# Regrouping a feed-forward layer that multiplies with seven products instead of eight

## The chip, the cores and the metric

The kernel runs on one core of one Trainium2 chip. The metric is device time in microseconds (us) of the whole program; the median of three runs before the change is 3438.2 us (3434.52 to 3442.72).

## The reference, cut to what matters

One layer of a hybrid decoder over 2048 prompt tokens and 64 sample tokens of width 1024, all in float32. The change touches the SwiGLU feed-forward that follows the output projection `h + mix @ w_out`:

```python
gu = rmsnorm(h, prm['norm2_g'][li]) @ prm['w_ffn_in'][li]
h = h + (jax.nn.silu(gu[..., :D_FF]) * gu[..., D_FF:]) @ prm['w_ffn_out'][li]
```

`D_FF` is 2816, that is 22 tiles of 128 features, each with a gate and an up part. After it come a gated per-layer input and a final norm.

## The kernel before

The prompt is worked on in four blocks of 512 tokens, counted from 0; block 3 also carries the 64 sample tokens. Everything is planned ahead: a scheduler simulates the program and fixes the order of instructions on each engine from priorities and data dependence, and tiles come from pools with a fixed number of buffers, whose reuse makes the next writer wait for the last reader. Token mixers (attention, recurrences) run beside the projections on the same engines, with lower priority. The sample tokens' mixers are placed beside block 2's last part.

Every matrix product is made of float32 operands split in a high part and a low rest (`split` L291 for activations, `unit` L268 and `parts` L688 for weights): ACT casts the high part, DVE or POOL subtracts it. Three matmuls (high-high, high-low, low-high) then replace one. High and low parts of weights live in two pools of seven buffers each, `whi` and `wlo` (L200, L201), raw weights in four buffers `wraw`. All weight loads are issued on SP's queue.

Blocks 0 and 1 use `rest` (L483), which the change leaves alone. Blocks 2 and 3 use `rest7` (L571): it splits the mixers' output (`mixed` L604), multiplies with `w_out` (`out_mm` L434, whose results are added to the residual rows h by DVE, L582), normalizes, runs the feed-forward `ffn7` (L622), and ends with a per-layer stage (L540).

`ffn7` splits the tokens in two halves (256 or 288 columns) and the 1024 rows of the contraction in two halves too, and computes gate and up of a feature tile together as a 2x2 block product. `seven` (L679) does that with seven block products instead of eight (twelve matmuls each, `prod` L712), from sums and differences of weights (four on DVE, L696) and of activations. The activations' sums are called t1 to t4, the plain blocks b11, b21, b12, b22. `Halves` (L103) makes them: PE transposes the scaled rows (L134), ACT multiplies by the gain into F (L139, L141), `split` makes the parts of the first token half; `second` (L153) makes those of the second half and t1 to t4 (subtractions on DVE, L164). Since t1 to t4 need both halves, the first feature tile is computed directly (`mm_half` L670, 96 matmuls): its first token half runs while the second is prepared. In one bank z, y or x a later product is added to an earlier one after DVE has read the earlier state:

```python
        prod(x, a11, ops["b11"], True)
        nc.scalar.copy(s, x)
        prod(z, s1, ops["t1"], True)
        tt(v, z, s, ALU.add)
        prod(y, s2, ops["t2"], True)
        tt(u, y, s, ALU.add)
        prod(x, a12, ops["b21"], False)
        prod(y, s3, ops["t3"], False)
```

After each feature tile ACT's tanh (L653) and two operations on DVE (L654, L655) give gate times up, and `split` (L296, L297) gives the tile `g`. Feature tiles are taken in groups: one tile first, then seven groups of three. After each group `out_mm` (matmuls on L364) multiplies the group's g with its rows of `w_ffn_out`, 512 output columns at a time, row tile by row tile, and DVE adds the result to h (L582). The last group's projection is interleaved with the norm of the per-layer stage.

Of the kernel before, what the change touches and what calls it, by code (L numbers as in the profile page):

```python
# [23 lines left out]
TB = 512  # L24
# [6 lines left out]
EPS = 1e-6  # L31
COL = {n: i * 256 for i, n in enumerate("aq af ai ag bq bk bv cq ck cv cz".split())}
# [4 lines left out]
class Norm:  # L37
# [33 lines left out]
    def steps(self):  # L71

        S, nc, acts, gain = self.S, self.S.nc, self.acts, self.gain
        for j, group in enumerate(self.groups):
# [6 lines left out]
            for k in range(KT):  # L81
                with S.at(0):
                    ps = S.bank()[:, :n]
                    for i, s in enumerate(xs):
                        nc.tensor.transpose(ps[:, i * rows:(i + 1) * rows], s[:, k * 128:(k + 1) * 128],  # L85
                                            S.ident[:rows, :rows])
                    S.split(acts[k][:, :, t0:t0 + n], ps, gain[:, k:k + 1])
                yield group[-1] if k == KT - 1 else None
# [14 lines left out]
class Halves(Norm):  # L103
# [4 lines left out]
    def __init__(self, S, h, gain, with_s, fp, sa):  # L108
# [3 lines left out]
        self.rows, self.ready, self.done = {}, {}, set()  # L112
        self.w = (TBS if with_s else TB) // 2
        self.f = [fp.tile([128, 2 * self.w], F32, name="F") for _ in range(KT)]
# [6 lines left out]
    def steps(self):  # L121
        S, nc, w = self.S, self.S.nc, self.w
        for j, group in enumerate(self.groups):
# [3 lines left out]
            for k in (0, 4, 1, 5, 2, 6, 3, 7):  # L127
                with S.at(0):
# [15 lines left out]
                yield  # L144

# [7 lines left out]
    def second(self, sb):  # L153
# [4 lines left out]
        nc = S.nc  # L158
        self.b22 = []

        self.b12 = [t[:, i] for t in (S.gp.tile([128, 2, 2, self.w], F32R, name="g", tag="g") for _ in range(2))
                    for i in range(2)]
        self.t = {n: [] for n in ("t1", "t2", "t3", "t4")}
        sub = lambda o, x, y: nc.vector.tensor_tensor(o, x, y, op=ALU.subtract)  # L164
        for k in range(4):
            b11, b12, b21, b22 = (self.part(a, j) for a, j in ((k, 0), (k, 1), (k + 4, 0), (k + 4, 1)))
            d = sb.tile([128, 2, self.w], F32R, name="Sb")
            self.b22.append(d)
            S.split(d, b22)
            tmp = S.xsp.tile([128, D], F32, name="xs")  # L170
            t1, t2, t3 = (tmp[:, i * self.w:(i + 1) * self.w] for i in range(3))
            sub(t1, b12, b11)
            sub(t3, b22, b12)
            sub(t2, b22, t1)
            S.split(self.b12[k], b12)
            sub(b21, b21, t2)
            for n, x in (("t1", t1), ("t2", t2), ("t3", t3), ("t4", b21)):
                d = sb.tile([128, 2, self.w], F32R, name="Sb")
                self.t[n].append(d)
                S.split(d, x)  # L180

    def half(self, j):
        if not j:
            return self.b11 + self.b21
        return self.b12 + self.b22

    def operands(self, sb):
        return {"b11": self.b11, "b21": self.b21, "b22": self.b22, **self.t}


class Step:
# [99 lines left out]
    def split(self, dst, src, scale=None):  # L291
# [3 lines left out]
        if scale is None:  # L295
            nc.scalar.copy(hi, src)  # L296
            nc.vector.tensor_tensor(lo, src, hi.bitcast(F32), op=ALU.subtract)  # L297
# [136 lines left out]
    def out_mm(self, acts, w, nk, n, with_s, use, norm=None, by_tile=False):  # L434
# [13 lines left out]
        for c, i, u in order:  # L448
            use(i, c, self.mm_a(acts, u, nk, i * 128, NS if i == 4 else 128, n))
# [121 lines left out]
    def rest7(self, b, mix, smix):  # L571
# [4 lines left out]
        w0 = (TBS if with_s else TB) // 2  # L576
# [7 lines left out]
        with pool("h7", 5 if with_s else 4) as self.hp, pool("g7", 3) as self.gp, ExitStack() as ops:  # L584
            ws, fp, sa = (ops.enter_context(pool(n, m)) for n, m in (("ws", 2), ("F", KT), ("Sa", KT)))
            with pool("pad", 1) as pad, pool("W", KT) as wp:
                if not with_s:
                    pad.tile([128, 1400], F32, name="pad")
# [4 lines left out]
                norm = Halves(self, h, self.gain["norm2_g"], with_s, fp, sa)  # L593
                self.out_mm(acts, I["w_out"][0], KT, 256, with_s, add, norm)
            last = self.ffn7(add, norm, ops.enter_context(pool("Sb", 20)), ws, with_s, w0)
            ops.close()
            with pool("L", KT) as lp:
# [3 lines left out]
                self.out_mm(*last, 512, with_s, add, norm, True)  # L601
# [20 lines left out]
    def ffn7(self, add, norm, sb, ws, with_s, w0):  # L622
# [3 lines left out]
        KC = 3  # L626
        f0 = 0
        while f0 < FT:
            n = KC if f0 else FT % KC
            gs = []  # L630
            for f in range(f0, f0 + n):
                wg, wu = (wi[:, c0:c0 + 128] for c0 in (f * 128, D_FF + f * 128))
                th = self.ev.tile([128, TBS], F32, name="ev")
                if f:
                    pairs = self.seven(wg, wu, ops, ws, w0)
                else:

                    us = [self.units([w], KT, 4) for w in (wg, wu)]
                    norm.first()
                    pairs = []  # L640
                    for j in range(2):
                        if j:
                            norm.second(sb)
                        if w0 == 256:
                            t = self.bank()
                            ps = [t[:, :w0], t[:, w0:]]
                        else:
                            ps = [self.bank()[:, :w0] for _ in us]
# [1468 lines left out]
```

## Time and profile before

| | |
|---|---|
| median of three runs | 3438.2 us |
| the profiled execution | 3437.55 us |
| its span, first to last instruction | 3435.7 us |
| mean granted TensorE clock | 0.978 |
| busy: PE / DVE / ACT / POOL | 3302.0 / 2254.7 / 1379.3 / 820.7 us |

PE is TensorE's matmuls, PEld its weight loads, DVE is VectorE, ACT is ScalarE, POOL is GpSimd, SP is SyncE, which issues the loads. L364 is line 364 of the kernel. An operation is written as output<-inputs, then its output and input shapes, then xN for a run of N. A figure in square brackets is idle time ahead of an instruction and what ended it. The granted clock is a share of 2.4 GHz. Times on PE are of pipelined matmuls, so starts tell more than durations.

### The profile page before, as it was taken

The numbers are of one execution on the slowest core, as the hardware profiler recorded it, in microseconds if no ns is written. First come the engines' busy times: TensorE is split into PE (matmuls) and PEld (weight loads), VectorE is DVE, ScalarE is ACT, GpSimd is POOL, SyncE is SP. The second block draws the span as 40 slices with busy tenths as digits, with TensorE's granted clock in tenths as the row PEclk, the third lists the DMA queues.
The fourth block names the chain that finished last, engine by engine and source line by source line (L and its number), as shares of the span: only waits on it lengthen the run. The fifth ranks groups of instructions, "written<-read, shape, count | busy, mean of one in ns | idle before, by whom it ended". The sixth has DMA issues, their size and how long they took to land.

```text
span 3435.7 us, 66579 instructions
## 1 busy us (share of the span) xinstructions
PE 3302.0 (96%) x24742; PEld 2815.2 (82%) x24742; DVE 2254.7 (66%) x6002; ACT 1379.3 (40%) x2931; POOL 820.7 (24%) x696
## 2 busy tenths in 40 slices
PE   7999999999999999998999999999999999899998
PEld 6788997888887778788878776787888889788988
DVE  4455566544577756688775455446799875877875
ACT  4433445324344224345333334535343453433443
POOL 2212122122112222212122212122334432233431
PEclk9999999999999999999999999999999999999999
DMA  6645445544433332534432443463533344122222
GB/s 207 181 121 149 127 123 155 148 125 145 129 109 118 101 96 87 132 91 146 113 103 81 124 114 110 143 215 113 162 102 88 91 129 134 60 81 90 83 89 79
DMA packets 621769, 411.92 MB, mean 120 GB/s; under 512 B 155357, under 2 KB 572877, under 8 KB 621445
## 3 DMA queue, kind: packets, MB, share of 16 engines
q1 hardware_dynamic: 618184, 405.12, 40.8%
q8 instruction: 195, 3.19, 0.4%
q10 hardware_dynamic: 3260, 2.55, 0.3%
q14 instruction: 130, 1.06, 0.1%
HBM read 348.77 MB, written 61.18 MB: 119 GB/s over the span
## 4 chain that ended last, share of the span: by engine, by line
PE 72%; DVE 13%; DMA 6%; SPq 4%; issue 3%; ACT 2%; POOL 1%; DVEq 0%; ACTq 0%; POOLq 0%
PE mmp L364 25%; PE mmp L344 22%; PE mmp L715 9%; SPq L1321 2%; PE acc L1852 1%; DVE c_X L1312 1%; DVE c_tmp L1310 1%; DMA wraw<-w_ffn_in 1%; DVE wlo L283 1%; PE mx L1135 1%; PE mx L1707 1%; PE mmp L85 1%; PE mx L1653 1%; PE mx L1764 1%; PE mx L1047 1%
## 5 line engine op out<-in xcount | busy, mean ns | idle before, releaser
L283 POOL TENSOR_TENSOR wlo<-wraw,whi 128x512 fp32r<-128x512 f32 (+1 forms) x356 | 497.5, 1399 | 1763.0 <-ACT whi L280 1112.8
L344 PE MATMUL mmp<-act,whi 128*128 128x512 f32 (+1 forms) x2944 | 892.7, 384 | 7.6 <-ACT ev L368 5.0
L280 ACT CAST whi<-wraw 128x512 fp32r<-128x512 f32 (+1 forms) x712 | 436.4, 619 | 667.4 <-PE mmp L344 240.6
L344 PEld LDWEIGHTS mmp<-act,whi 128*128 128x128 f32 x2944 | 532.9, 190 | 111.9 <-ACT ev L368 6.8
L364 PE MATMUL mmp<-whi,act 128*128 128x256 f32 (+3 forms) x2992 | 574.8, 290 | 11.8 <-DVE act L297 6.9
L344 PE MATMUL mmp<-act,wlo 128*128 128x512 f32 (+1 forms) x1472 | 554.0, 383 | 0.0
L364 PE MATMUL mmp<-whi,g 128*128 128x512 f32 (+1 forms) x1496 | 491.2, 406 | 15.4 <-DVE h L492 5.8
L364 PEld LDWEIGHTS mmp<-whi,act 128*128 128x128 f32 (+1 forms) x2992 | 470.8, 190 | 21.5 <-DVE act L297 7.8
L364 PE MATMUL mmp<-wlo,act 128*128 128x256 f32 (+2 forms) x1496 | 431.0, 289 | 0.2 <-DVE wlo L283 0.2
L283 DVE TENSOR_TENSOR wlo<-wraw,whi 128x512 fp32r<-128x512 f32 (+1 forms) x356 | 279.9, 787 | 219.0 <-ACT whi L280 198.3
L692 POOL TENSOR_TENSOR wlo<-wraw,whi 128x512 fp32r<-128x512 f32 x168 | 243.6, 1453 | 468.6 <-ACT whi L691 411.8
L364 PEld LDWEIGHTS mmp<-whi,g 128*128 128x128 f32 (+1 forms) x1496 | 273.3, 188 | 95.5 <-ACT g L296 8.5
L715 PE MATMUL mmp<-Sb,whi 128*128 128x256 f32 (+1 forms) x1680 | 328.0, 292 | 7.2 <-DVE xs L696 5.8
L344 PEld LDWEIGHTS mmp<-act,wlo 128*128 128x128 f32 x1472 | 276.4, 190 | 50.2 <-issue 2.0
L364 PE MATMUL mmp<-wlo,g 128*128 128x512 f32 x748 | 297.6, 400 | 0.0
L364 PEld LDWEIGHTS mmp<-wlo,act 128*128 128x128 f32 (+1 forms) x1496 | 283.5, 190 | 4.0 <-issue 2.0
L715 PEld LDWEIGHTS mmp<-Sb,whi 128*128 128x128 f32 x1680 | 267.0, 190 | 12.7 <-DVE xs L696 8.4
L715 PE MATMUL mmp<-Sb,wlo 128*128 128x256 f32 (+1 forms) x840 | 241.7, 291 | 1.8 <-POOL wlo L692 1.8
L691 ACT CAST whi<-wraw 128x512 fp32r<-128x512 f32 x210 | 128.8, 619 | 229.1 <-PE mmp L364 94.5
L364 PEld LDWEIGHTS mmp<-wlo,g 128*128 128x128 f32 x748 | 140.2, 187 | 33.7 <-issue 0.5
L715 PEld LDWEIGHTS mmp<-Sb,wlo 128*128 128x128 f32 x840 | 159.0, 190 | 3.4 <-POOL wlo L692 2.2
L582 DVE TENSOR_TENSOR h<-mmp,h 128x512 f32<-128x512 f32 (+3 forms) x180 | 107.6, 630 | 72.0 <-PE mmp L364 65.5
(472 smaller groups left out, 5250.1 us busy)
## 6 DMA issues: line engine op xcount, KB each, us to landing
wraw<-w_ffn_in SPq DMA_DIRECT2D x352, 256.0 KB
wraw<-w_in SPq DMA_DIRECT2D x208, 256.0 KB
wraw<-w_ffn_out SPq DMA_DIRECT2D x176, 256.0 KB
wraw<-w_out SPq DMA_DIRECT2D x64, 256.0 KB
wraw<-w_ple_gate SPq DMA_DIRECT2D x64, 256.0 KB
bs_K<-cache_b_k SPq DMA_DIRECT2D x48, 256.0 KB
xs<-x_prompt SPq DMA_DIRECT2D x16, 512.0 KB
h<-x_prompt SPq DMA_DIRECT2D x16, 512.0 KB
```

The lines of the kernel that those rows point to most:

```text
L85: nc.tensor.transpose(ps[:, i * rows:(i + 1) * rows], s[:, k * 128:(k + 1) * 128], S.ident[:rows, :rows])
L280: nc.scalar.copy(hi, raw)
L283: eng.tensor_tensor(lo, raw, hi.bitcast(F32), op=ALU.subtract)
L344: nc.tensor.matmul(ps, u[a], acts[k][:, b, t:t + w], start=i == 0, stop=i == n)
L364: nc.tensor.matmul(ps, acts[k][:, b, t0:t0 + rows], units[k][a], start=i == 0, stop=i == n)
L582: nc.vector.tensor_tensor(d, ps, d, op=ALU.add)
L691: nc.scalar.copy(hi, x)
L692: eng.tensor_tensor(lo, x, hi.bitcast(F32), op=ALU.subtract)
L715: nc.tensor.matmul(ps, w[a][:, k], op[k][:, b], start=first and k == 0 and j == 0, stop=k == 3 and j == 2, skip_group_check=True)
L1047: nc.tensor.matmul(ss[:, k:k + 2], x[:, c, t * m:(t + 1) * m], M.blk2, start=True, stop=True)
L1135: nc.tensor.matmul(ps[64 * hp:64 * hp + ms, ct, n], k[r, ct, 64 * n:64 * n + ms], part(q[r, ct, 64 * n:64 * n + 64], 1), start=True, stop= ...
L1321: nc.sync.dma_start(out=xt[r, ct, n], in_=xd[:, hp, ct, n, d].rearrange("k j i -> j k i"))
```

## The change

- The 22 feature tiles go in groups of 4, 5, 5, 5 and 3, and the first two (`LEAD`) are computed directly: first halves of both, then second halves of both.
- In `Halves`, the gain of rows 512 to 1023 is applied by DVE instead of ACT; the sample tokens stand in the middle of the columns, after row tile 1, so one operation scales a whole group of rows, and g is split by one pair of instructions. `out_mm` gets `mid`, which finds the row tiles there.
- `second` first splits b12 and b22 of all four k, then makes t1 to t4; the rest of t3 is subtracted by POOL; t4 takes t1's scratch.
- In `seven` the second product comes from t2 and the fourth from t1; the parts are made in another order, with s2 on DVE and a12 on POOL.
- The pool of F is shared with t1 to t4 of k = 2, 3; the pool `Sb` has 12 buffers instead of 20, the pool of g five instead of three; a padding tile is gone.

```diff
-    def __init__(self, S, h, gain, with_s, fp, sa):
+    ORDER = (0, 4, 1, 5, 2, 6, 3, 7)
+
+    def __init__(self, S, h, gain, with_s, sa, sf):
...
-        self.f = [fp.tile([128, 2 * self.w], F32, name="F") for _ in range(KT)]
+        self.f = {k: sf.tile([128, 2 * self.w], F32, name="F", tag="Sb") for k in self.ORDER}
...
-                    g, f = self.gain[:, k:k + 1], self.f[k]
-                    t0 = j * w
-                    m = w if n > 256 else 256
-                    nc.scalar.mul(f[:, t0:t0 + m], ps[:, :m], g)
-                    if n > m:
-                        nc.scalar.mul(f[:, 2 * w - n + m:], ps[:, m:], g)
+                    g, f = self.gain[:, k:k + 1], self.f[k][:, t0:t0 + n]
+                    if k < 4:
+                        nc.scalar.mul(f, ps, g)
+                    else:
+                        nc.vector.tensor_scalar_mul(f, ps, g)
...
+        new = lambda p: p.tile([128, 2, w], F32R, name="Sb", tag="Sb")
+        for k in range(4):
+            S.split(self.b12[k], self.part(k, 1))
+            self.b22.append(new(sb))
+            S.split(self.b22[k], self.part(k + 4, 1))
         for k in range(4):
             b11, b12, b21, b22 = (self.part(a, j) for a, j in ((k, 0), (k, 1), (k + 4, 0), (k + 4, 1)))
-            d = sb.tile([128, 2, self.w], F32R, name="Sb")
-            self.b22.append(d)
-            S.split(d, b22)
...
             sub(t1, b12, b11)
+            sub(t2, b22, t1)
             sub(t3, b22, b12)
-            sub(t2, b22, t1)
-            S.split(self.b12[k], b12)
-            sub(b21, b21, t2)
-            for n, x in (("t1", t1), ("t2", t2), ("t3", t3), ("t4", b21)):
-                d = sb.tile([128, 2, self.w], F32R, name="Sb")
-                self.t[n].append(d)
-                S.split(d, x)
+            for n, x in (("t1", t1), ("t2", t2), ("t3", t3), ("t4", t1)):
+                if n == "t4":
+                    sub(x, b21, t2)
+                self.t[n].append(new(sb if k < 2 else self.sf))
+                S.split(self.t[n][k], x, nc.gpsimd if n == "t3" else None)
...
-            use(i, c, self.mm_a(acts, u, nk, i * 128, NS if i == 4 else 128, n))
+            t0 = i * 128 if not mid or i < 2 else 256 if i == 4 else i * 128 + NS
+            use(i, c, self.mm_a(acts, u, nk, t0, NS if i == 4 else 128, n))
...
-        with pool("h7", 5 if with_s else 4) as self.hp, pool("g7", 3) as self.gp, ExitStack() as ops:
-            ws, fp, sa = (ops.enter_context(pool(n, m)) for n, m in (("ws", 2), ("F", KT), ("Sa", KT)))
-            with pool("pad", 1) as pad, pool("W", KT) as wp:
-                if not with_s:
-                    pad.tile([128, 1400], F32, name="pad")
+        with pool("h7", 5 if with_s else 4) as self.hp, pool("g7", 5) as self.gp, ExitStack() as ops:
+            ws, sa, sf = (ops.enter_context(pool(n, m)) for n, m in (("ws", 2), ("Sa", KT), ("Sf", KT)))
+            with pool("W", KT) as wp:
...
-            last = self.ffn7(add, norm, ops.enter_context(pool("Sb", 20)), ws, with_s, w0)
+            last = self.ffn7(add, norm, ops.enter_context(pool("Sb", 12)), ws, with_s)
...
+        for n in (4, 5, 5, 5, 3):
             gs = []
...
+            if not f0:
+
+                us = [[self.units([w], KT, 4) for w in cols(f)] for f in range(LEAD)]
+                norm.first()
+                pairs = [[] for _ in us]
+                for j in range(2):
+                    if j:
+                        norm.second(sb)
+                    for u, p in zip(us, pairs):
+                        p.append([self.mm_half(ps, w, norm.half(j)) for ps, w in zip(bank2(2), u)])
+                gs = [glu(p) for p in pairs]
+                ops = norm.operands()
+            gs += [glu(self.seven(*cols(f), ops, ws, w0)) for f in range(f0 + len(gs), f0 + n)]
             w = wo[f0 * 128:(f0 + n) * 128]
             f0 += n
             if f0 < FT:
-                self.out_mm(gs, w, n, 512, with_s, add)
+                self.out_mm(gs, w, n, 512, with_s, add, mid=with_s)
...
-        s1 = parts(s, V)
         tt(u1, g1, u1)
         tt(g1, s, g1)
-        s2 = parts(g1, G)
-        a12 = parts(g2, V)
+        s2 = parts(g1, V)
+        a12 = parts(g2, G)
+        s1 = parts(s, V)
...
-        x, z, y = (self.bank()[:, :w0] for _ in range(3))
+        x, y, z = (self.bank()[:, :w0] for _ in range(3))
...
-        prod(z, s1, ops["t1"], True)
-        tt(v, z, s, ALU.add)
         prod(y, s2, ops["t2"], True)
         tt(u, y, s, ALU.add)
         prod(x, a12, ops["b21"], False)
+        prod(z, s1, ops["t1"], True)
+        tt(v, z, s, ALU.add)
         prod(y, s3, ops["t3"], False)
```

## Rows read from the trace of the kernel before

**Rows 1.** The page, busy time, share of the span and instructions of each engine.
```profile
PE 3302.0 (96%) x24742; PEld 2815.2 (82%) x24742; DVE 2254.7 (66%) x6002; ACT 1379.3 (40%) x2931; POOL 820.7 (24%) x696
```
**Rows 2.** Busy time by stretches (us, PE, PEld, DVE, ACT, POOL, clock, DMA, GB/s).
```profile
2346.00:2396.00 50.00, 42.89 (x382) 34.10 (x383) 37.22 (x100) 33.93 (x79) 5.90 (x4) 0.93 0.35 102
2396.00:2787.00 391.00, 373.37 (x2800) 329.29 (x2798) 326.22 (x659) 162.16 (x324) 156.18 (x110) 0.99 0.41 116
2917.00:2960.00 43.00, 30.20 (x164) 25.56 (x164) 38.11 (x93) 25.13 (x69) 5.68 (x5) 0.80 0.13 37
2960.00:3345.00 385.00, 381.22 (x2388) 341.83 (x2388) 298.84 (x481) 154.46 (x310) 143.24 (x103) 1.00 0.29 87
```
**Rows 3.** PE's pace: stretches of 256 and 288 columns; timeline, 512 columns.
```profile
2880.00:2900.00 20.00, 20.00 (x172) 20.00 (x171) 5.83 (x12) 3.09 (x5) 2.92 (x2) 1.00 0.36 109
2960.00:2980.00 20.00, 20.00 (x152) 20.00 (x152) 14.47 (x24) 8.99 (x18) 9.30 (x7) 1.00 0.23 67
...
3171.03 0.39 PE L364 MATMUL mmp<-wlo,g 128*128 128x512 f32 x1
...
3179.36 0.62 PE L364 MATMUL mmp<-whi,g 128*128 128x512 f32 x2
```
**Rows 4.** Timeline of PE, two boundaries before a down projection in block 3.
```profile
3110.83 0.69 PE L364 MATMUL mmp<-whi,g 128*128 128x512 f32 x2 [0.17 <-ACT whi L691]
...
3166.45 0.70 PE L364 MATMUL mmp<-whi,g 128*128 128x512 f32 x2 [0.18 <-ACT whi L691]
...
3170.22 0.50 PE L364 MATMUL mmp<-whi,g 128*128 128x512 f32 x1 [0.38 <-DVE g L297]
```
**Rows 5.** Timeline of PE, block 3's opening: pauses, first seven-product tile.
```profile
2924.80 0.69 PE L134 MATMUL mmp<-ident,xs 128*128 128x128 f32 x2 [2.49 <-ACT F L141]
...
2928.32 1.97 PE L134 MATMUL mmp<-ident,xs 128*128 128x128 f32 x8 [2.83 <-DVE xs L68]
...
2946.10 0.40 PE L676 MATMUL mmp<-Sb,whi 128*128 128x288 f32 x1 [2.80 <-DVE Sb L297]
...
2949.74 3.35 PE L364 MATMUL mmp<-whi,g 128*128 128x512 f32 x7 [2.85 <-ACT g L296]
...
2959.16 0.43 PE L715 MATMUL mmp<-Sb,whi 128*128 128x288 f32 x2
```
**Rows 6.** Busy time by stretches within the two openings, columns as in rows 2.
```profile
2360.00:2370.00 10.00, 8.28 (x69) 6.48 (x70) 7.73 (x26) 6.12 (x16) 0.00 (x0) 0.66 0.31 90
...
2917.00:2930.00 13.00, 5.85 (x30) 4.13 (x29) 11.47 (x33) 10.02 (x31) 2.25 (x2) 0.65 0.21 61
...
2950.00:2955.00 5.00, 5.00 (x13) 3.77 (x13) 3.02 (x6) 0.00 (x0) 0.00 (x0) 0.51 0.27 77
```
**Rows 7.** Groups of instructions by shape, 2917 to 2946 (busy us, mean ns | idle).
```profile
L139 ACT ACTIVATE F<-mmp,gcol 128x288 f32<-128x288 f32 x8 | 3.7, 531 | 0.0
...
L141 ACT ACTIVATE F<-mmp,gcol 128x32 f32<-128x32 f32 x8 | 2.0, 339 | 0.0
...
L297 DVE TENSOR_TENSOR Sa<-F,Sa 128x288 fp32r<-128x288 f32 x8 | 3.4, 452 | 0.0
```
**Rows 8.** DVE's weight sums: one in the timeline, and their group (2960 to 3327).
```profile
3161.99 0.69 DVE L696 TENSOR_TENSOR ws<-wraw 128x512 f32<-128x512 f32 x1 [1.29 <-DMA wraw<-w_ffn_in]
...
L696 DVE TENSOR_TENSOR ws<-wraw 128x512 f32<-128x512 f32 x39 | 47.3, 1214 | 18.3 <-DMA wraw<-w_ffn_in 18.1
```
**Rows 9.** Block 2, 2396 to 2787: waits (total, times, longest); DVE's adds to h.
```profile
PE mmp L715 <- DVE xs L696: 5.5, 10, 1.7
...
PE mmp L364 <- ACT g L296: 1.1, 3, 0.5
...
L582 DVE TENSOR_TENSOR h<-mmp,h 128x512 f32<-128x512 f32 x54 | 35.1, 681 | 7.0 <-PE mmp L364 6.9
```
**Rows 10.** Groups of ACT and POOL, block 3's long stretch (2960 to 3327): weight parts.
```profile
L691 ACT CAST whi<-wraw 128x512 fp32r<-128x512 f32 x100 | 61.9, 620 | 126.1 <-PE mmp L364 57.9 <-issue 24.2 <-DVE wraw L696 19.7
...
L692 POOL TENSOR_TENSOR wlo<-wraw,whi 128x512 fp32r<-128x512 f32 x81 | 110.1, 1359 | 217.6 <-ACT whi L691 191.9 <-PE mmp L715 23.4 <-DVE wlo L692 1.9
```

More of the change, by code (lines that the diff above doesn't have):

```diff
@@ L86, in steps @@
                                             S.ident[:rows, :rows])
-                    S.split(acts[k][:, :, t0:t0 + n], ps, gain[:, k:k + 1])
+                    S.split(acts[k][:, :, t0:t0 + n], ps, scale=gain[:, k:k + 1])
                 yield group[-1] if k == KT - 1 else None
@@ L126, in steps @@
             n = sum(self.ready[i].shape[0] for i in group)
-            for k in (0, 4, 1, 5, 2, 6, 3, 7):
+            for k in self.ORDER:
                 with S.at(0):
@@ L157, in second @@
             pass
-        nc = S.nc
+        nc, w = S.nc, self.w
         self.b22 = []
-        self.b12 = [t[:, i] for t in (S.gp.tile([128, 2, 2, self.w], F32R, name="g", tag="g") for _ in range(2))
+        self.b12 = [t[:, i] for t in (S.gp.tile([128, 2, 2, w], F32R, name="g", tag="g") for _ in range(2))
                     for i in range(2)]
@@ L431, in in_proj, with out_mm @@
         return after
-    def out_mm(self, acts, w, nk, n, with_s, use, norm=None, by_tile=False):
+    def out_mm(self, acts, w, nk, n, with_s, use, norm=None, by_tile=False, mid=False):
         cols = [slice(c0, c0 + n) for c0 in range(0, D, n)]
@@ L600, in rest7 @@
                 norm = self.norm(lambda i: (h[i], False), self.gain["ple_norm_g"], with_s, scale=False, ahead=False)
-                self.out_mm(*last, 512, with_s, add, norm, True)
+                self.out_mm(*last, 512, with_s, add, norm, True, mid=with_s)
                 self.per_layer_out(b, h, norm, pa, pas)
@@ L620, in mixed, with ffn7, bank2, glu @@
         return acts
-    def ffn7(self, add, norm, sb, ws, with_s, w0):
+    def ffn7(self, add, norm, sb, ws, with_s):
         nc, I = self.nc, self.I
         wi, wo = I["w_ffn_in"][0], I["w_ffn_out"][0]
-        KC = 3
+        w0 = norm.w
+        def bank2(n):
+            if 2 * w0 > TB:
+                return [self.bank()[:, :w0] for _ in range(n)]
+            t = [self.bank() for _ in range((n + 1) // 2)]
+            return [t[i // 2][:, i % 2 * w0:(i % 2 + 1) * w0] for i in range(n)]
+        def glu(pairs):
+            th = self.ev.tile([128, TBS], F32, name="ev")
+            for j, (gate, up) in enumerate(pairs):
+                e = th[:, j * w0:(j + 1) * w0]
+                nc.scalar.activation(e, gate, AF.Tanh, scale=0.5)
+                nc.vector.scalar_tensor_tensor(e, e, 1.0, gate, op0=ALU.add, op1=ALU.mult)
+                nc.vector.scalar_tensor_tensor(e, e, 0.5, up, op0=ALU.mult, op1=ALU.mult)
+            g = self.gp.tile([128, 2, 2 * w0], F32R, name="g", tag="g")
+            self.split(g, th[:, :2 * w0])
+            return g
+        cols = lambda f: [wi[:, c0:c0 + 128] for c0 in (f * 128, D_FF + f * 128)]
@@ L627, in ffn7 @@
         f0 = 0
-        while f0 < FT:
-            n = KC if f0 else FT % KC
+        for n in (4, 5, 5, 5, 3):
             gs = []
[L631 to L648, printed above, removed]
-                        pairs.append([self.mm_half(p, u, norm.half(j)) for p, u in zip(ps, us)])
-                    ops = norm.operands(sb)
-                for j, (gate, up) in enumerate(pairs):
-                    e = th[:, j * w0:(j + 1) * w0]
-                    nc.scalar.activation(e, gate, AF.Tanh, scale=0.5)
-                    nc.vector.scalar_tensor_tensor(e, e, 1.0, gate, op0=ALU.add, op1=ALU.mult)
-                    nc.vector.scalar_tensor_tensor(e, e, 0.5, up, op0=ALU.mult, op1=ALU.mult)
-                g = self.gp.tile([128, 2, 2 * w0], F32R, name="g", tag="g")
-                gs.append(g)
-                halves = th[:, :2 * w0].rearrange("p (j n) -> p j n", j=2)
-                for c, m in ((0, 256), (256, w0 - 256)):
-                    if m:
-                        self.split(g[:, :, 2 * c:2 * (c + m)].rearrange("p a (j n) -> p a j n", j=2),
-                                   halves[:, :, c:c + m])
```

22 lines of the change are left out of this document (11 added, 11 removed).

## The prediction

> **What bounds the kernel now.** I read the page's busy times first, then busy time by stretches of the part that the change touches, then the timeline at PE's pauses, then waits and instruction groups. The page says that PE is busy for 96% of the span and no other engine for over 66% [rows 1]. The change touches only the two blocks that use seven products. Blocks are counted from 0: block 2 runs its feed-forward from 2346 to 2787 us, block 3 (with the sample tokens) from 2917 to 3345. So only what PE loses in these 870 us can come back. In four stretches [rows 2] the reader is to see that losses sit in the two openings (7.1 us idle of 50 in block 2, 12.8 of 43 in block 3) and in block 2's long stretch (17.6 of 391), while block 3's long stretch is nearly full (3.8 of 385).
>
> Busy time hides a second loss: a matmul counts as busy while it is slow. So I take PE's undisturbed pace [rows 3]: 172 matmuls of 256 columns in 20 us (0.1163 us each), 152 of 288 columns in 20 us (0.1316), and 36 starts of 512 columns from 3171.03 to 3179.36 (0.2314). With these, one period of three tiles in block 3 should take 252 x 0.1316 + 90 x 0.2314 = 54.0 us; the timeline shows 55.6 from one boundary to the next (3110.83 to 3166.45) [rows 4]. The missing 1.6 us lie where PE turns from a seven-product tile to the down projection and waits for the last tile's g. There are six such boundaries per block, and a seventh before the last projection.
>
> In block 3's opening [rows 5] PE waits 2.49 us for ACT's F, 2.83 for the scaled rows xs, 2.80 for an operand part Sb and 2.85 for the first g. Right after these pauses the granted clock is 0.65 and 0.51 of 2.4 GHz, that is near the 1.2 GHz level, and in block 2's opening 0.66 [rows 6]: ten microseconds at 2360 hold 69 matmuls.
>
> **The change, part by part.** The sum is made against the profiled execution, 3437.55 us (span 3435.7), which is 0.65 below the median of the runs.
>
> *Second direct tile.* A direct tile has 96 matmuls, a seven-product tile 84. Twelve more cost 12 x 0.1163 = 1.4 us in block 2 and 1.6 in block 3. What it buys is cover: first halves of two tiles instead of one (96 matmuls, 12.6 us in block 3) run while second-half operands are made.
>
> *Opening of block 3.* Before, the norm part takes 13 us (2917 to 2930) with ACT busy 10.0 and DVE 11.5 [rows 6]. ACT loses its eight 32-column scalings (0.34 each) and four of the wide ones (0.53) [rows 7], 4.8 us; DVE gains four scalings. Those aren't shown on DVE; the nearest rows are its other 288-column operations at 0.45 [rows 7], so 2 us, against which weight sums at 0.69 [rows 8] move behind the direct tiles. ACT alone would give 4 us, DVE alone might cost 1; I take 1 us gained, since DVE has the fewer free slices. Then 192 direct matmuls, 25.3 us. DVE was busy 38.1 of the 43 us [rows 2] and still has nearly all of it to do, so I leave 3 us of waiting before the first seven-product tile (0 to 6). It would start at 2917 + 12 + 25.3 + 3 = 2957.3. Before, it starts at 2959.16 [rows 5] with one direct tile and its 30 down matmuls done; put on equal work that is 2959.16 + 84 x 0.1316 - 30 x 0.2314 = 2963.3. Gain 6 us, the extra matmuls within it. With ACT's 4 us and no waiting it would start at 2951.3, with DVE's 1 us of loss and 6 of waiting at 2962.3: bounds 12 and 1.
>
> *Opening of block 2.* It loses 7.1 us idle [rows 2] and some 3 to the low clock [rows 6], partly from the sample mixers, which stay. I take 4 of these back, bounds 0 and 8, minus the 1.4 us of matmuls.
>
> *Groups of 4, 5, 5, 5, 3.* Two boundaries fewer per block. Block 3: 2 x 1.6 = 3.2 us, bounds 0 and 9 (a longer group has more k steps to do before the last g is needed, so the others may shrink too). In block 2 waits on g are 1.1 us in three [rows 9]: I take 1 us, bounds 0 and 2. Evacuations fall by 24 per block in block 2 and 30 in block 3, 0.68 us of DVE each [rows 9]. In block 3 that hides under PE. In block 2 DVE is busy 326 of 391 us [rows 2] and PE's longest list of waits there is for DVE's sums xs (5.5 us in 10) [rows 9]. 16 us of adds and some 6 of weight work go; I take 4 us back, bounds 0 and 8. The first projection's two loads of 256 KB move on SP's queue behind those of three more tiles, where they are needed later too; POOL's queue is passed by nothing.
>
> *Order of products, engines of the parts.* Nothing. The bank y has one product more of cover before its third product, z three fewer before its last; each order has two one-product covers. DVE and POOL make as many parts as before. If DVE's queue is late, z is what waits next, at the 0.5 us a wait of [rows 9]. *Sample tokens in the middle*: one split per g instead of two, 22 short pairs less on ACT and DVE, hidden beside PE except at the boundaries already counted. *Pools*: operands of k = 2, 3 take over the buffers of F, whose last readers stand ahead of them on DVE; no wait, and if one came it would hold only DVE's split for 0.45 us.
>
> *Third operands' parts go from DVE to POOL.* A DVE subtraction of weights takes 0.69 us alone, but 1.21 on average beside POOL's parts (1.36 each) [rows 8, 10]. I count neither gain nor loss (bounds 2 us either way, inside the opening's). The Trainium skill ("SBUF — State Buffer", Who interferes with whom) says that a VectorE instruction with two SBUF inputs blocks fully against a GpSimd one that reads SBUF; the trace's stretched mean agrees, and by that rule the move would relieve DVE of nothing.
>
> Sum: -6 - (4 - 1.4) - 3.2 - 1 - 4 = -16.8; 3437.55 - 16.8 = **3420.8 us**.
>
> **Rivals.**
> *DVE is the bound of the openings.* For: 38.1 of 43 us busy, and the subtractions held by POOL. Against: PE's pauses name ACT and PE's own queue order too. The openings would give 1 us in block 3 and nothing in block 2, DVE no relief: 3437.55 - 1 - 3.2 - 1 + 1.4 = 3433.8. The Trainium skill's rule on the shared port (above) would lead here.
> *All waits of these kinds go.* The upper ends, shaved by a quarter since they don't add up fully: 12 + 8 + 9 + 2 + 8 - 1.4 = 37.6, so 28 us, 3409. For: block 2's DVE load falls by 7%. Against: sample mixers' waits stay.
> *Seven weight buffers are too few* (the slow side). Two direct tiles need eight pairs of whi and wlo where there are seven, a projection of five tiles ten, one of four eight; before, six. For the second column half, the third part can only be made once the last row tile of the first half lets go of its first. PE then has 18 matmuls of cover, 4.2 us; ACT's cast plus POOL's subtraction take 0.62 + 1.36 [rows 10], so it decides where a cast starts over 2 us late. ACT's casts already wait for PE [rows 10]. Price: 2 us at each of two turns in eight groups, 32 us, giving 3437.55 - 16.8 + 32 = 3453; slower from 12 of the 16 turns on. Against: the output projection before (256-column stretch of [rows 3]) also refills its buffers in flight, and runs without a pause.
> *It doesn't do what it says*: PE's order is fixed ahead of the run, and if it puts the second halves where they were, all stays at about 3437.
>
> **How the numbers follow.** My forecast has 0.55, DVE's bound 0.18, all waits 0.12, the buffers 0.10, no effect 0.05. A measurement of this kernel can tell 0.2% (6.9 us) from no change, so faster means below 3431.3. The forecast's own range, with two of its larger terms at their ends, is 3411 to 3430. Faster: 0.55 + 0.12 + a third of DVE's case (it lies 2.5 us above the line) = 0.73. Same: the other two thirds and no effect, 0.17. Slower: the buffers, 0.10. The range reaches from 3406 (all waits) to 3434 (DVE's case); the buffers, no effect and a tail of the lower case are left out.
>
> **What would show it.** Right: no pause over 1 us before the first seven-product tile of block 3, which starts some 41 us after its last output projection; two direct tiles ahead of it; a granted clock of 1.00 there; four boundaries of some 1.6 us; fewer waits for xs in block 2. Wrong: waits of PE on whi or wlo in the middle of a down projection (buffers), DVE without idle time in the opening and PE waiting for Sb ahead of the seven products (DVE's bound), or a start of block 3 that is no earlier than before.

## The result, and the profile after

The changed kernel takes 3471.0 us (median of four runs, 3462.7 to 3476.7). The kernel before took 3438.2 beside it. The ratio is 1.0093 [1.0067, 1.0119], so the change costs 0.9% where a gain of 0.5% was forecast. The profiled execution took 3476.67 us. The page of the changed kernel, span and busy times:

```profile
span 3474.9 us, 66460 instructions
...
PE 3321.5 (96%) x24766; PEld 2827.4 (81%) x24766; DVE 2205.7 (63%) x5914; ACT 1362.8 (39%) x2877; POOL 819.6 (24%) x700
```

Against [rows 1] DVE has 49 us less to do and PE 24 matmuls more, as foreseen, and still the span is 39 us longer. (9.6 of it lie ahead of block 2's norm, where no instruction changed; see the last section.) The stretches that answer to [rows 2], same columns: opening and seven products of block 2, then of block 3.

```profile
2356.00:2408.00 52.00, 47.28 (x442) 40.38 (x443) 37.35 (x98) 32.27 (x72) 13.39 (x9) 0.93 0.35 101
2408.00:2799.00 391.00, 365.67 (x2699) 318.88 (x2698) 300.70 (x614) 152.73 (x309) 146.01 (x106) 0.97 0.38 109
2934.00:2981.50 47.50, 39.26 (x281) 37.63 (x280) 42.56 (x113) 26.16 (x62) 13.63 (x9) 0.89 0.11 32
2981.50:3367.00 385.50, 365.22 (x2265) 326.29 (x2264) 257.77 (x396) 138.19 (x261) 138.31 (x99) 1.00 0.28 85
```

The openings improved: PE is idle 4.7 and 8.2 us where it was 7.1 and 12.8, although they now hold two direct tiles. The long stretches are where the time went: in block 3 PE now idles 20.3 of 385.5 us, before 3.8 of 385, while DVE's busy share there falls from 78% to 67%. PE's waits between the first and the last seven-product matmul of block 3 (total, times, longest), after the change:

```profile
PE mmp L715 <- DVE xs L696: 18.8, 17, 2.6
PE mmp L715 <- POOL wlo L692: 1.1, 3, 0.6
PE mmp L367 <- DVE ev L640: 0.3, 1, 0.3
```

and the same view of the kernel before:

```profile
PE mmp L364 <- DVE g L297: 1.9, 5, 0.4
PE mmp L364 <- ACT whi L691: 0.9, 5, 0.2
PE mmp L715 <- DVE xs L696: 0.3, 1, 0.3
```

20.2 us against 3.1. From its first seven-product matmul to the end block 3 takes 3474.9 - 2981.5 = 493.4 us; before it took 3435.7 - 2959.2 = 476.5, on equal work (one tile of 11.05 us less, 30 down matmuls of 0.2314 more) 472.4. So 17.1 of the 21.0 us lost are these waits. PE waits for DVE's adds of a product out of a bank (xs), although DVE is less loaded.

For the lines that follow: a tile's four raw weight buffers hold two gate blocks g1, g2 and two up blocks u1, u2. DVE makes s = u1 + u2, then u1 = g1 - u1 and g1 = s - g1 in place, and later s = g2 - g1 in the same buffer s (pool `ws`). The parts (ACT's high cast, and the low rest on DVE or POOL) of the first s are s1, of the new g1 s2, of the new u1 s3, of the second s s4; a12 and a22 are those of g2 and u2. DVE's timeline over one tile of block 3 shows what stands ahead of the adds:

```profile
3162.08 0.69 DVE L696 TENSOR_TENSOR ws<-wraw 128x512 f32<-128x512 f32 x1 [1.35 <-DMA wraw<-w_ffn_in]
3162.69 0.45 DVE L696 TENSOR_TENSOR xs<-mmp,xs 128x288 f32<-128x288 f32 x1
...
3163.42 0.68 DVE L696 TENSOR_TENSOR wraw<-wraw 128x512 f32<-128x512 f32 x1
3164.21 0.69 DVE L696 TENSOR_TENSOR wraw<-ws,wraw 128x512 f32<-128x512 f32 x1
...
3166.22 1.77 DVE L692 TENSOR_TENSOR wlo<-wraw,whi 128x512 fp32r<-128x512 f32 x1
3167.91 1.77 DVE L692 TENSOR_TENSOR wlo<-ws,whi 128x512 fp32r<-128x512 f32 x1
3169.61 0.45 DVE L696 TENSOR_TENSOR xs<-mmp,xs 128x288 f32<-128x288 f32 x1
3169.97 0.68 DVE L696 TENSOR_TENSOR ws<-wraw 128x512 f32<-128x512 f32 x1
3171.39 0.69 DVE L692 TENSOR_TENSOR wlo<-ws,whi 128x512 fp32r<-128x512 f32 x1 [0.74 <-ACT whi L691]
...
3176.26 0.83 DVE L696 TENSOR_TENSOR ws<-wraw 128x512 f32<-128x512 f32 x1 [1.83 <-DMA wraw<-w_ffn_in]
...
3177.38 0.44 DVE L696 TENSOR_TENSOR xs<-mmp,xs 128x288 f32<-128x288 f32 x1
```

PE's pauses in the same microseconds, and POOL's rests beside the two long ones of DVE:

```profile
3163.19 0.53 PE L715 MATMUL mmp<-Sb,whi 128*128 128x288 f32 x2 [1.69 <-DVE xs L696]
...
3170.11 0.53 PE L715 MATMUL mmp<-Sb,whi 128*128 128x288 f32 x2 [1.27 <-DVE xs L696]
...
3177.88 0.40 PE L715 MATMUL mmp<-Sb,whi 128*128 128x288 f32 x1 [1.64 <-DVE xs L696]
...
3166.15 2.98 POOL L692 TENSOR_TENSOR wlo<-wraw,whi 128x512 fp32r<-128x512 f32 x2 [4.09 <-ACT whi L691]
```

Read it as a round. 3162.08 is the first sum, u1+u2, which waited for its load. The two other sums follow, then the rests of s2 and s1, 1.77 us each, and only then, at 3169.97, the difference g2-g1 (also `ws<-wraw`): it is written into s, which s1's parts still read. The difference gives the raw buffers of g1 and g2 back; the loads of the next tile follow, and its first sum starts at 3176.26. That is 7.89 us from sum to difference, 6.29 from difference to sum, a round of 14.2 us; the two rounds before it in this group take 12.4 and 13.4. PE needs 84 x 0.1316 = 11.05 us for a tile [rows 3]. Each time DVE stands at the sum for a load, or in the two long rests, an add queued behind it comes late and PE pauses: of the 17 waits, 11 (13.1 us) end with an add that stands behind a sum that waited for its load, and six (5.7 us) with one right behind the two rests. That the loads wait for the difference shows on SP's queue, over the same stretch of block 3, after and then before the change:

```profile
SPq L685 <- DVE ws L696: 173.8, 14, 18.0
```

```profile
SPq L685 <- DVE ws L696: 91.4, 13, 9.0
```

The same three instructions in the kernel before:

```profile
3128.05 0.69 DVE L696 TENSOR_TENSOR ws<-wraw 128x512 f32<-128x512 f32 x1 [1.00 <-DMA wraw<-w_ffn_in]
...
3132.31 1.74 DVE L696 TENSOR_TENSOR ws<-wraw 128x512 f32<-128x512 f32 x1
...
3140.10 1.11 DVE L696 TENSOR_TENSOR ws<-wraw 128x512 f32<-128x512 f32 x1 [0.22 <-DMA wraw<-w_ffn_in]
```

There the difference comes 4.26 us after the sum, since s1's parts are made second, and the round is 12.05 us.

### The profile page after: what moved, and what is told of

Read it like the earlier page. It is cut to its first block, busy times and chain, and to the rows that moved or that the text cites. A ratio compares the mean times of both kernels' runs of the same rounds, so it can differ in the third digit from the quotient of the medians.

```text
span 3474.9 us, 66460 instructions
## 1 busy us (share of the span) xinstructions
PE 3321.5 (96%) x24766; PEld 2827.4 (81%) x24766; DVE 2205.7 (63%) x5914; ACT 1362.8 (39%) x2877; POOL 819.6 (24%) x700
## 5 line engine op out<-in xcount | busy, mean ns | idle before, releaser
L367 PE MATMUL mmp<-whi,g 128*128 128x512 f32 (+1 forms) x1496 | 484.0, 403 | 8.7 <-DVE h L496 5.3
L715 PE MATMUL mmp<-Sb,whi 128*128 128x256 f32 (+1 forms) x1600 | 319.4, 296 | 30.5 <-DVE xs L696 28.2
L692 POOL TENSOR_TENSOR wlo<-wraw,whi 128x512 fp32r<-128x512 f32 x160 | 228.2, 1433 | 391.3 <-ACT whi L691 318.9
L367 PE MATMUL mmp<-wlo,g 128*128 128x512 f32 (+1 forms) x748 | 296.5, 399 | 0.0
L715 PEld LDWEIGHTS mmp<-Sb,whi 128*128 128x128 f32 x1600 | 255.2, 192 | 42.9 <-DVE xs L696 37.8
L715 PE MATMUL mmp<-Sb,wlo 128*128 128x256 f32 (+1 forms) x800 | 229.8, 292 | 0.0
L691 ACT CAST whi<-wraw 128x512 fp32r<-128x512 f32 x200 | 120.8, 618 | 194.9 <-DVE wraw L696 92.8
L367 PEld LDWEIGHTS mmp<-wlo,g 128*128 128x128 f32 (+1 forms) x748 | 139.4, 186 | 34.5 <-POOL wlo L286 0.4
L585 DVE TENSOR_TENSOR h<-mmp,h 128x512 f32<-128x512 f32 (+3 forms) x126 | 74.2, 608 | 90.5 <-PE mmp L367 81.8
## 6 DMA issues: line engine op xcount, KB each, us to landing
xs<-x_prompt SPq DMA_DIRECT2D x16, 512.0 KB
h<-x_prompt SPq DMA_DIRECT2D x16, 512.0 KB
```

The source lines that it names most:

```text
L367: nc.tensor.matmul(ps, acts[k][:, b, t0:t0 + rows], units[k][a], start=i == 0, stop=i == n)
L585: nc.vector.tensor_tensor(d, ps, d, op=ALU.add)
L691: nc.scalar.copy(hi, x)
L692: eng.tensor_tensor(lo, x, hi.bitcast(F32), op=ALU.subtract)
L715: nc.tensor.matmul(ps, w[a][:, k], op[k][:, b], start=first and k == 0 and j == 0, stop=k == 3 and j == 2, skip_group_check=True)
```

## The experiments

Single profiles are compared by stages, because spans shift (last section): the time from the first norm transposes of block 2 to those of block 3, and from there to the end. `xs` is PE's wait for DVE's adds in block 3's seven products (us). Each ratio is to runs of the kernel before on the same chip at the same time, whose medians lay between 3438.2 and 3441.9 us.

| kernel | median us | ratio to before | block 2 | block 3 to end | xs |
|---|---|---|---|---|---|
| before | 3438.2 | 1 | 563.0 | 525.8 | 0.3 |
| after | 3471.0 | 1.0093 [1.0067, 1.0119] | 577.3 | 541.1 | 18.8 |
| e1_groups3 | 3457.7 | 1.0045 [1.0029, 1.0062] | 573.6 | 530.3 | 8.6 |
| e2_oldorder | 3447.9 | 1.0021 [1.0007, 1.0034] | 574.0 | 518.8 | 2.3 |
| e3_groups3_oldorder | 3435.8 | 0.9971 [0.9957, 0.9985] | 561.3 | 518.4 | 0 |
| e4_before_neworder | 3462.6 | 1.0055 [1.0033, 1.0076] | 570.6 | 531.2 | 5.6 |
| e5_before_newparts | 3445.8 | 1.0019 [1.0007, 1.0030] | 571.0 | 522.6 | 0.3 |
| e6_before_newproducts | 3431.1 | 0.9970 [0.9956, 0.9984] | 559.2 | 518.8 | 0.5 |
| e8_after_sum_on_pool | 3477.2 | 1.0109 [1.0091, 1.0127] | 582.9 | 544.7 | 24.8 |
| e9_own_diff | 3437.1 | 0.9983 [0.9966, 1.0] | 560.0 | 523.2 | 5.6 |
| e10_own_raw | 3458.6 | 1.0045 [1.0027, 1.0062] | 570.0 | 535.9 | 13.0 |
| e12_oldparts | 3440.1 | 1.0001 [0.9988, 1.0014] | 569.5 | 522.9 | 4.9 |
| e11_groups3_oldparts | 3431.2 | 0.9976 [0.9964, 0.9988] | 569.1 | 512.0 | 0 |
| e14_old_engines | 3468.2 | 1.0081 [1.0063, 1.0099] | 579.7 | 539.2 | 19.4 |
| e17_new_engines | 3437.7 | 0.9994 [0.9980, 1.0007] | 567.7 | 519.4 | 0.5 |
| e15_own_diff_groups3 | 3423.6 | 0.9948 [0.9930, 0.9965] | 559.0 | 513.0 | 0 |
| e16_groups3_oldparts_own | 3433.6 | 0.9976 [0.9964, 0.9987] | 570.5 | 512.6 | 0 |

**Which part of the change.** Four kernels take the groups and the two orders in `seven` (parts and products together) back, one by one and both, and put the new orders alone into the kernel before. The edits:

```diff
# e1 and e3: groups
-        for n in (4, 5, 5, 5, 3):
+        for n in (4, 3, 3, 3, 3, 3, 3):
# e2 and e3: parts and products as before (e4: the reverse, in the kernel before)
         tt(s, u1, u2, ALU.add)
+        s1 = parts(s, V)
...
-        s2 = parts(g1, V)
-        a12 = parts(g2, G)
-        s1 = parts(s, V)
+        s2 = parts(g1, G)
+        a12 = parts(g2, V)
...
-        x, y, z = (self.bank()[:, :w0] for _ in range(3))
+        x, z, y = (self.bank()[:, :w0] for _ in range(3))
...
+        prod(z, s1, ops["t1"], True)
+        tt(v, z, s, ALU.add)
         prod(y, s2, ops["t2"], True)
...
-        prod(z, s1, ops["t1"], True)
-        tt(v, z, s, ALU.add)
```

> The changed kernel with its feature tiles in groups of 4 and then six times 3; all else as changed. Theory 1 (a run of five seven-product tiles outruns the preparation of its weights, which a down projection every three tiles lets catch up): the 33 us lost in the seven-product stretches go, some 5 us come back for two more boundaries per block, so about 3443 us, and PE's waits for xs in block 3 fall from 18.8 us to under 5. Theory 2 (the new order of the parts makes the preparation of one tile longer, whatever the grouping): it stays above 3460.

> The changed kernel with parts and products of a seven-product tile in the order of before; groups of 4, 5, 5, 5, 3 kept. Theory 1 (length of the runs): hardly faster than the changed kernel, 3462 to 3471 us, waits for xs in block 3 above 12 us. Theory 2 (order of the parts): back to about 3438 us, and the last group, which has three tiles and lost some 5 us, runs as before.

> Both undone: groups of 4 and six times 3, old order of parts and products; the two direct tiles, the openings, the sample tokens in the middle and the pools stay as changed. If run length and order together are the whole loss, what is left is the openings' gain (5.7 us in block 3 and 1.4 in block 2, by the traces) and one boundary fewer per block: about 3428 to 3432 us. If something else of the change costs time (pools, the upstream part), it stays above 3438.

> The kernel before with only the new order of parts and products. Theory 1: within 4 us of before, 3434 to 3442. Theory 2: slower by 10 us or more, with waits for xs inside the groups of three.

The orders cost most: undone they give 0.7% in groups of five (e2), and alone they make the kernel before 0.55% slower (e4). The groups cost too, with either order. What is left without both (e3: openings, second direct tile, sample tokens in the middle, pools) is 0.3% faster than before. The undone groups (e1) gave less than the first of the two expectations and more than the second; e2 came back most of the way.

**Parts or products.** e5 and e6 split e4.

```diff
# e5: parts only, in the kernel before
-        s1 = parts(s, V)
...
-        s2 = parts(g1, G)
-        a12 = parts(g2, V)
+        s2 = parts(g1, V)
+        a12 = parts(g2, G)
+        s1 = parts(s, V)
# e6: products only, in the kernel before
-        x, z, y = (self.bank()[:, :w0] for _ in range(3))
+        x, y, z = (self.bank()[:, :w0] for _ in range(3))
...
-        prod(z, s1, ops["t1"], True)
-        tt(v, z, s, ALU.add)
         prod(y, s2, ops["t2"], True)
...
         prod(x, a12, ops["b21"], False)
+        prod(z, s1, ops["t1"], True)
+        tt(v, z, s, ALU.add)
```

> The kernel before with only the new order and engines of a tile's weight parts (s1 fourth, s2 on DVE, a12 on POOL); products in the old order. Theory A (the parts: the sum for s2 and the longer hold of raw buffers put DVE's weight sums ahead of their loads, and PE's xs sums wait behind them): most of the 20 us of the whole order, 3450 us or more on a chip where before is 3440, and DVE's waits for w_ffn_in in block 3 at 30 us or more (18 before). Theory B (the products: less cover for a bank's second use): within 4 us of before.

> The kernel before with only the new order of products and banks; parts made in the old order. Theory A: within 4 us of before, DVE's waits for w_ffn_in in block 3 about 18 us. Theory B: slower by 15 us or more, with PE's waits for xs above 5 us in block 3.

The new products gain 0.30%, the new parts lose 0.19%, and together they lose 0.55%: the effects don't add. The long round alone isn't enough, either. In block 3 the round from one tile's first sum to the next takes 13.3 us in e5 (3137.24 to 3150.53) and 13.4 in e4 (3150.33 to 3163.73), but PE waits 0.3 us for xs in e5 and 5.6 in e4, and e5's loss lies in block 2 alone. So the late difference costs together with the new order of products. As the program is written, that order leaves one product between the two uses of bank z where there were three, and one instead of two for x; that these thinner covers are why is argued and not shown. New parts with the old products in groups of five were not tried.

**First tries at the wait.** e7 gives `wraw` six buffers instead of four, e8 makes u1+u2 on POOL so that DVE need not stand at it.

```diff
# e7
-        self.wraw = pool("wraw", 4)
+        self.wraw = pool("wraw", 6)
# e8
-        tt(s, u1, u2, ALU.add)
+        tt(s, u1, u2, ALU.add, nc.gpsimd)
```

> The changed kernel with six raw weight buffers instead of four, nothing else. Theory A (loads come late because a raw buffer is let go late): loads start a tile's half earlier, DVE's waits for w_ffn_in in block 3 fall from 35 us to under 10 and 15 us or more come back: at or under 3455. Theory B or a limit in ACT, DVE and POOL themselves (the parts of one tile take longer than its products): no more than 5 us come back, and DVE's waits move to another releaser.

> The changed kernel with the first weight sum of a tile (u1 + u2) on POOL instead of DVE, so that a late load holds POOL's queue and not the queue that also holds PE's xs sums. Theory A: PE's waits for xs in block 3 fall from 18.8 us to under 8 and 10 us or more come back, although POOL takes some 0.7 us longer per sum. If the wait in DVE's queue is only a sign of a late load and not the cause, PE waits as long, for parts instead of xs, and the time stays within 5 us of the changed kernel.

e7 took 3718.0 us (1.0808 [1.0792, 1.0825]), and its whole time says nothing on the question: with six buffers the order of instructions differs from the start of the program, from 2375 to 2580 us of its span (columns as above) PE works on the sample tokens' mixers alone, at a granted clock of 0.50, and block 2's output projection follows from 2584 us on.

```profile
2375.00:2580.00 205.00, 127.15 (x1026) 67.62 (x1024) 11.66 (x30) 34.65 (x49) 6.95 (x29) 0.50 0.41 117
```

Its block 3 can be compared by the stage: 539.0 us to the end, 16.6 us of waits for xs and 29.7 us of DVE's waits for loads, against 541.1, 18.8 and 36.0 in the changed kernel. Two more buffers in the common pool do not repair it.

e8 is no faster, which looked like evidence against DVE's queue. Its waits of DVE in block 3's seven products tell otherwise:

```profile
DVE wraw L696 <- POOL ws L696: 38.8, 18, 5.2
```

The next sum on DVE overwrites u1, which POOL's sum reads, so the wait only moved by one instruction; in the changed kernel it was 36.0 us in 19 for the load. The load or its sum stays ahead of the adds either way.

**What makes the round long.** e9 gives the difference a buffer of its own and, as this allows, makes it right after the three sums; e10 gives g1 and g2 raw buffers of their own (two tiles fit instead of one), e12 takes the parts back and keeps the products, e11 is e12 in groups of three. None changes an instruction ahead of block 2's feed-forward.

```diff
# e9
+            self.ws2 = ops.enter_context(pool("ws2", 2))
...
-        s = ws.tile([128, 4, 128], F32, name="ws")
+        s, d = ws.tile([128, 4, 128], F32, name="ws"), self.ws2.tile([128, 4, 128], F32, name="ws", tag="ws")
...
         tt(g1, s, g1)
+        tt(d, g2, g1)
...
-        tt(s, g2, g1)
-        s4 = parts(s, V)
+        s4 = parts(d, V)
# e10
+            self.raw7 = ops.enter_context(pool("raw7", 4))
...
-            raw[n] = self.wraw.tile([128, 4, 128], F32, name="wraw")
+            raw[n] = (self.raw7 if n[0] == "g" else self.wraw).tile([128, 4, 128], F32, name="wraw", tag="wraw")
# e12 (and e11, with e1's groups)
+        s1 = parts(s, V)
...
-        s2 = parts(g1, V)
-        a12 = parts(g2, G)
-        s1 = parts(s, V)
+        s2 = parts(g1, G)
+        a12 = parts(g2, V)
```

> The changed kernel, but the difference of weights g2 - g1 has a buffer of its own and is made right after the three sums, not after the parts of s1. Theory L (a loop of weight buffers): a tile's raw weights can only be loaded when the tile before has given its raw buffers back, and the last event of that on DVE is the difference. In the changed kernel's block 3 the loop is 6 us from the difference to the next tile's first sum (three loads) plus 6 to 8 us from the sum to the difference, 12.3 to 15.3 together, against the 11.05 us in which PE works a tile off; with the old order of parts it is 11.9. Here the sum should be followed by the difference in some 3 us, the loop be 10 us or less, PE's waits for xs in block 3 fall from 18.8 to under 5 us, and the time from 3471 to about 3452 (3443 to 3460). Theory P (the order of the products alone makes DVE's adds come too late, whatever the weights do): waits for xs stay at 15 us or more, 3465 to 3475.

> The changed kernel, but the raw weights g1 and g2 of a seven-product tile have four buffers of their own, so that raw weights of two tiles fit instead of one; the order of parts and products stays. Theory L: the loop then spans two tiles and bounds nothing; DVE's waits for loads in block 3 (36 us) fall by half or more, PE's waits for xs from 18.8 to under 6 us, and the time to about 3452 (3443 to 3460). Theory P: DVE waits less for loads but PE's waits for xs stay over 12 us, 3463 to 3475.

> The changed kernel with the parts made in the old order and on the old engines, but the products in the new order (groups of 4, 5, 5, 5, 3 kept). Theory L: the time from the sum to the difference goes back to about 4.8 us, the loop to 11.9; waits for xs in block 3 under 5 us, 3442 to 3454. Theory P: the products are the fault, so the time stays over 3460.

> As the kernel before this one, and in groups of 4 and six times 3. Theory L: like the changed kernel with both orders and the groups undone (3435.8), less what the new products gave in the kernel before (8 us): 3424 to 3436, the fastest of all. Theory P: 3445 to 3458.

One more buffer, with the earlier place that it allows, takes the whole loss away (e9, 3437.1, less than the 3443 to 3460 expected). DVE's timeline in e9, from a first sum to the next:

```profile
3115.19 1.10 DVE L696 TENSOR_TENSOR ws<-wraw 128x512 f32<-128x512 f32 x1 [1.88 <-DMA wraw<-w_ffn_in]
...
3119.18 0.68 DVE L696 TENSOR_TENSOR ws<-wraw 128x512 f32<-128x512 f32 x1
3119.78 0.68 DVE L692 TENSOR_TENSOR wlo<-wraw,whi 128x512 fp32r<-128x512 f32 x1
...
3121.12 1.05 DVE L692 TENSOR_TENSOR wlo<-ws,whi 128x512 fp32r<-128x512 f32 x1
...
3126.51 1.03 DVE L696 TENSOR_TENSOR ws<-wraw 128x512 f32<-128x512 f32 x1 [2.25 <-DMA wraw<-w_ffn_in]
```

The difference now stands ahead of both rests, 3.99 us after the sum, and the round is 11.3 us (one later in each group is 13.5). DVE's own waits for loads are no shorter than before the repair, 41.3 us against 36.0; but only one of PE's eight waits, of 0.2 us, ends with an add that follows a sum that waited for its load. e12 does the same by order (4.55 and 11.6 us) and ends at 3440.1. So the new products are not at fault by themselves. e10 fell short: DVE's waits for loads halve (36.0 to 15.3 us) as expected, but xs stays at 13.0 and only 12 of 34 us come back (by the ratios, 17 of 38). Three of its 15 waits (3.0 us) still end with an add behind a late load. The raw buffers are therefore a part of it alone. In e10 the difference still follows s1's rest, and s4's cast and rest (with a 0.74 us wait for ACT's cast) follow it, ahead of the adds; that this is the other part is read from its timeline and was not tried by itself.

**Order or engines, groups, and the best version.** e14 and e17 split e12; e15 is e9 in e1's groups; e16 is e11 with e9's buffer.

```diff
# e14
-        s2 = parts(g1, V)
-        a12 = parts(g2, G)
+        s2 = parts(g1, G)
+        a12 = parts(g2, V)
# e17
         tt(s, u1, u2, ALU.add)
+        s1 = parts(s, V)
...
-        s1 = parts(s, V)
```

> The changed kernel, with s2's rest back on POOL and a12's on DVE, and the order of the parts left new (s1 last of the four). Theory B (the shared buffer): the difference still has to wait until both parts of s1 are made, since it overwrites s, so little changes: 3460 to 3475, waits for xs in block 3 over 12 us. Theory E (the engines): a12 is needed one product later than s2, so DVE and POOL are relieved at the right place: 3440 to 3452.

> The changed kernel, with s1's parts back in second place, and the new engines kept (s2 on DVE, a12 on POOL). Theory B: s is free early, the difference follows the sums, 3438 to 3450 and waits for xs in block 3 under 7 us. Theory E: 3460 to 3475.

> The changed kernel with a buffer of its own for the difference, in groups of 4 and six times 3. If groups of five cost only because a tile's preparation is slower than PE (the round of 12.3 to 15.3 us against 11.05), they cost little now: 3432 to 3440, at most 5 us under the same kernel in the change's groups (3437). If they cost by themselves (longer bursts of weights, later down projections), 3422 to 3430.

> New products, old order and engines of the parts, the difference in a buffer of its own, groups of 4 and six times 3. If in this order the shared buffer holds nothing up any more (block 3 shows no waits of PE at all there, and s is given back early), the buffer adds nothing: 3428 to 3434, like the same kernel without it (3431). If the two repairs add up: 3420 to 3427.

The engines don't matter (e14 stays slow, with 7.9 us from sum to difference), the place of s1's parts does (e17, 4.2 us). e16 gains nothing over e11, so the two repairs are one. e15 is faster than both kernels, 0.52% under the one before. Groups of five still cost there: 0.35% between e9 and e15. PE's waits in block 3's seven products of e9, and of e15:

```profile
PE mmp L715 <- DVE xs L696: 5.6, 8, 1.4
PE mmp L715 <- DVE wlo L692: 1.9, 3, 0.6
```

```profile
PE mmp L367 <- DVE xs L696: 0.2, 1, 0.2
```

(The last line is a wait of a down projection's matmul.) These 7.3 us are most of the 10.2 that block 3 gains. In a group of five even e9's rounds (11.3 to 13.5 us) are longer than PE's 11.05, and the next pause for the weights' preparation, a down projection, comes after five tiles instead of three. That this is what the groups cost is shown by waits for block 3 of this pair alone. Between e2 and e3 block 3 is alike (518.8 and 518.4 us) and the difference lies in block 2 (574.0 and 561.3); some of it is the clock's, since e2's block 2 has 17 us more at the 1.2 GHz level of the granted clock (30.7 against 13.7), worth about half of that by the estimate of the last section.

## Why the prediction was wrong

- **Order of products, engines of the parts: "Nothing."** This is the step that failed. I counted instructions per engine, rightly, and did not follow the buffer s: its second writer now stands behind s1's parts, and s1 is made last. Worth about 34 us by the medians (after against e9) and 38 by the ratios. The covers were miscounted, too: z keeps one product of three before its last use and x one of two before its second, so there are three one-product covers where there were two. By themselves the new products gained 0.30% (e6), so that slip alone does not explain the loss.
- **Groups: -3.2, -1 and DVE's relief of -4.** Wrong in sign. In four pairs (after and e1, e2 and e3, e12 and e11, e9 and e15) the groups of five cost 0.48, 0.50, 0.25 and 0.35%. The waits at the boundaries of block 3 did vanish (no wait of PE for g after the change, 1.9 us in five before), but with the rest of the change and not by the groups: e15, in groups of three, has none either. DVE did have less to do; it was its order that mattered, not its load.
- **Opening of block 3, -6.** The size is right: it measured 5.7, and the first seven-product tile starts 40.8 us after the last matmul of the output projection (2940.7), as foreseen. From the first transposes to the first seven-product matmul it took 2981.5 - 2933.8 = 47.7 us. Before it was 2959.2 - 2909.9 = 49.3, plus 84 x 0.1316 for the second tile, minus 30 x 0.2314 for the down matmuls already done, 53.4. The second tile's cover did what was expected: PE no longer waits for operand parts or for the first g (2.80 and 2.85 us before), and the clock is 1.00 from 2960 us to the first seven-product tile. The split of the sum is luck in part: 3 us of waiting were counted there, none came, and all 8.2 us of waits lie in the norm instead, 6.0 of them in one wait for the sum of squares (ss).
- **Opening of block 2, -4 + 1.4.** 1.4 us gained by the same reckoning, half of the 2.6 forecast.
- **The rivals.** Slower was foreseen for too few buffers of weights, with a chance of 0.10 and 3453. The kind was right, the place wrong: within the down projections PE waited for a high part for 1.6 us in two waits in block 2 and not at all in block 3, and the scarce buffer was not one of the seven of whi and wlo but the shared `ws`. DVE as the bound of the openings foresaw a gain of 1 us in block 3's and none in block 2's, where 5.7 and 1.4 came; in the long stretch, where PE waits for it, DVE is busy for 67%.
- **The skill's rule weighed there**, that a VectorE instruction with two SBUF inputs contends with a GpSimd one that reads SBUF (the Trainium skill, "SBUF — State Buffer", Who interferes with whom), fits the rows after: two rests of 1.77 us each beside POOL's at 3166.15, where a later one takes 0.69. It decides nothing by itself: e9 keeps the same instructions on the same engines.

Open remain: block 2 lost 15.7 us behind its opening by the same reckoning, and PE's waits explain 8 of them (24.6 us against 16.6 in its seven products). The granted clock stands at the 1.2 GHz level for 20.4 us there where it was 13.7, worth some 3 us by the estimate of the last section. The sample mixers are woven in between in another order. In e9 block 2 is 17.3 us shorter than after the change, with 8.9 us less of PE's waits (1.7 of them for xs) and 10 us less at the 1.2 GHz level; how the buffer brings that about was not traced. The mechanism is shown in block 3. The 0.3% of the new products (e6) were not traced: 2.6 us of its 7 in block 3 are waits. Whether groups of four would do better was not tried.

## What to carry to other kernels

When parts of a tile are reordered, follow each scratch buffer to its next writer: a reused buffer can move an early instruction behind late ones, and with it the release of every buffer that instruction reads. How much that costs depends on how long the main engine can do without the instructions queued behind it. Write the preparation of a tile as a round (load, first use, last use, release, next load) and compare it with the time the main engine needs for a tile; an engine at 67% busy can still be late. Before grouping more tiles between two pauses of the main engine, check that this round is the shorter of the two.

## What the runs showed that I had not expected

- Ahead of block 2's feed-forward the order of instructions is the same in all kernels of the table, yet the first transposes of its norm start at 2346.9 us before, 2356.5 after, and between 2343.7 (e12) and 2360.6 (e4) over all: 17 us that no edit made. They go with the granted clock: ahead of that point it stands at the 1.2 GHz level for 99 us in e12, 106 before, 130 after and 133 in e4, so 34 us more at that level go with 17 us of time, half of them. The runs of one kernel show the same: the changed kernel took 3462.7 us at a mean granted clock of 0.980 and 3476.7 at 0.975. Two profiles are compared by the lengths of stages, and these too are a few us apart by the clock.
- Two more raw buffers (e7) cost 247 us without touching the inner loop: block 2 no longer began beside the sample mixers, and PE ran them alone at a granted clock of 0.50.
- A wait that is moved to another engine can stay as long as it was: e8 exchanged 36.0 us of waiting for a load for 38.8 us of waiting for POOL.
